# Thirty-five seven-product quads instead of twenty-six, with GpSimd making their sums, in an fp32 hybrid attention and state-space block

## The chip, the core and the metric

The kernel runs on one core of a Trainium2 chip. The time is the device time of one execution, in microseconds (us): the median of the runs, each a whole pass from inputs in device memory to the output. The core has five engines that run side by side, each with its own queue of instructions in a fixed order: TensorE (PE: matmuls; PEld: the loads of their stationary operand), VectorE (DVE), ScalarE (ACT), GpSimd (POOL) and SyncE (SP, which here only issues transfers). They wait for each other by semaphores.

## The reference

One block of a hybrid network on x of 256 rows and 2048 columns, in fp32:

```
hn   = rms_norm(x, norm_w)
q, k, v, z_a, z_s, xbc, dt, g_a, g_s = split(hn @ w_in)
o_a  = dilated_window_attention(q, k, v, three patterns) * silu(z_a)
y    = rms_norm(ssd_scan(conv(xbc), dt) * silu(z_s), ssm_norm_w)
m    = sigmoid(g_a) * (o_a @ w_attn_branch) + sigmoid(g_s) * (y @ w_ssm_branch)
out  = rms_norm(x + m @ w_out, final_norm_w)
```

The weights are about 63 million fp32 numbers, read once each; what takes the time is the matmuls with them.

## The kernel before, in words

**Three matmuls for one.** An fp32 product is made of operands split in a high part (what the matmul format keeps; ScalarE's copy) and a low part (VectorE's subtraction of the high part from the whole). A product is high x high + high x low + low x high: the helper `triple`, three matmuls of 128 x 128 with 512 columns. The activations are split once; every weight tile is split when it comes in. Weights come in units of 128 x 1024 (tag `w`, four buffers), and each unit's parts go to tiles `h` and `l` (four buffers each). `unit` does this for the plain case, lines 214 to 228.

**Phases.** First the projections for the state-space branch and its scan, then five large products in `gemm_pair` and others in `gemm_a` and `gemm_b`: ssm (4096 deep, output columns in two calls, 0 and 2, of 1024 each), v (columns 0 and 2), the gate ga (columns 2), then the attention heads with their projections, then attn (columns 0 in `gemm_pair`) and out (columns 0 and 2, in `gemm_pair`).

**Quads.** `gemm_pair` walks over the depth in steps of 2 x 128, a quad: two row blocks of the output by two column blocks of 512 by two depth blocks. A plain quad is 2 x 2 x 2 products, 24 matmuls. A quad listed in `S_QUADS` is made with seven products instead of eight (Strassen's way, in Winograd's form), 21 matmuls. For this its weights are stored in another order (units wa and wb), and sums are needed on both sides:

- of the weights: t13 (1024 wide, line 426), then two 512-wide sums in place in wb (lines 431 and 432). Four sets of high and low parts follow: a of wa, c of half of wb, t of t13, u of wb. The sets a and c take tiles from the ring `h`/`l` of four, t and u from a second ring `ht`/`lt` of two in the pool `mul`.
- of the left factor (activations): `turn_x`, lines 342 to 363: one sum of 512 columns, four of 128, then the split into `sx`. It is made once for each depth position and used by all calls that list it. Its temporary lies in a tile of its own.

Four accumulators hold the plain part, four more the extra products; `fold` (line 452) brings the latter together at a call's end, with two copies by ScalarE and four additions by VectorE.

**What sets the order.** A scheduler places the instructions of each engine at build time by its own model of their times; weight preparation is given a high priority (`L_AHEAD`), so that it runs ahead of the matmuls as far as buffers allow. On the chip each engine then keeps that order, whatever the real times are.

Of the kernel before, what the change touches and what calls it, by code (L numbers as in the profile page):

```python
# [9 lines left out]
F32 = mybir.dt.float32  # L10
F32R = mybir.dt.float32r
# [161 lines left out]
def hybrid_block(ctx: ExitStack, tc: tile.TileContext, wall, xt, x, pk_d, cst_d, fw_d, out):  # L173
# [33 lines left out]
    def load(n, cuts=(0, UNIT)):  # L207
        if n not in loaded:
            loaded[n] = stream.tile([P, UNIT], F32, name=f"w{n}", tag="w", bufs=W_BUFS)
        for a, b in zip(cuts, cuts[1:]):  # L210
            nc.sync.dma_start(loaded[n][:, a:b], wall[n, :, a:b])

    def unit(n, shape):
        if n not in loaded:
            load(n)
        w = loaded.pop(n)
        h = stream.tile([P, UNIT], F32R, name=f"h{n}", tag="h", bufs=H_BUFS)
        l = stream.tile([P, UNIT], F32R, name=f"l{n}", tag="l", bufs=H_BUFS)
        cuts = (0, UNIT // 2, UNIT) if n < N_FINE else (0, UNIT)
        with tc.high_priority(L_AHEAD) if n >= KT // UB else nullcontext():  # L220
            for a, b in zip(cuts, cuts[1:]):
                ac.activation(h[:, a:b], w[:, a:b], AF.Copy)  # L222
                ve.tensor_tensor(l[:, a:b], w[:, a:b], h[:, a:b].bitcast(F32), ALU.subtract)  # L223
# [117 lines left out]

    def turn_x(pool, bufs, temp, x, spare=0):


        sx = pool.tile([P, 2, 4 - spare, P], F32R, name=f"sx{now[0]}", tag="sx", bufs=bufs)
        a = temp[:, 0].rearrange("p (k i s) -> p k i s", k=2, i=2)
        s = temp[:, 1].rearrange("p (n s) -> p n s", n=4)
        xf = x.bitcast(F32)
        ve.tensor_tensor(a.rearrange("p k i s -> p k (i s)"), xf[:, :, :S], xf[:, :, S:], ALU.add)
        a11, a21, a12, a22 = a[:, 0, 0], a[:, 0, 1], a[:, 1, 0], a[:, 1, 1]  # L350
        ve.tensor_tensor(s[:, 0], a21, a22, ALU.add)
        ve.tensor_tensor(s[:, 1], a21, a11, ALU.subtract)
        ve.tensor_tensor(s[:, 2], s[:, 0], a11, ALU.subtract)
        ve.tensor_tensor(s[:, 3], a12, s[:, 2], ALU.subtract)
        parts = [(sx[:, 0, n], sx[:, 1, n]) for n in range(4 - spare)]
        if spare:
            own = x[:, 0, P:S], x[:, 0, S + P :]
            split(s[:, 0], *own)
            parts.insert(0, own)
        split(s[:, spare:], sx[:, 0], sx[:, 1])  # L360
        return parts

    def gemm_pair(tag, x_of, n_kt, sxs, swap, extra={}, close=1):
# [20 lines left out]
        for q in range(n_q):  # L384
# [27 lines left out]

            def hl(where, suffix, tags, bufs):
                return [
                    where.tile([P, UNIT], F32R, name=f"{t}{suffix}{n}", tag=t, bufs=bufs) for t in tags
                ]

            def part(src, h, l):
# [4 lines left out]
            with tc.high_priority(L_AHEAD):  # L423
                t13 = mul.tile([P, UNIT], F32, name=f"t13_{n}", tag="t13", bufs=1)
                b12 = wb[:, :512].unsqueeze(1).to_broadcast([P, 2, 512])
                ve.tensor_tensor(two(t13), b12, two(wa), ALU.subtract)
# [4 lines left out]
                ve.tensor_tensor(wb[:, :512], wa[:, 512:], t13[:, :512], ALU.subtract)  # L431
# [354 lines left out]
    mul = ctx.enter_context(tc.tile_pool(name="mul", bufs=1))  # L786
    mul.tile([P, MUL_PAD], F32, name="line", tag="line")

    def scale_gate():
# [17 lines left out]
    with tc.tile_pool(name="xp", bufs=1) as xp:  # L807
        sxs = {}
        for c in (0, 2):
            for q in S_QUADS[("ssm", c)]:  # L810
                if q not in sxs:
                    temp = xp.tile([P, 4, 512], F32, name=f"sxt_y{q}", tag="tmp", bufs=1)
                    sxs[q] = turn_x(xp, 6, temp, two_kts(yT[q // 8], q % 8), 1)
            es, prods = gemm_pair(
# [14 lines left out]
    sx_of_x = {}  # L829
    with tc.tile_pool(name="xt", bufs=1) as xtemp:  # L830
        for c in (0, 2):
            for q in S_QUADS[("v", c)]:
                if q not in sx_of_x:
                    temp = xtemp.tile([P, 2, 512], F32, name=f"sxt_x{q}", tag="tmp", bufs=1)
                    sx_of_x[q] = turn_x(xp, 3, temp, two_kts(XT, q))
            es, prods = gemm_pair(("v", c), lambda kt: XT[:, kt, :], KT, sx_of_x, c == 2)
            dst = blocks(vt, c)
            fold(prods, dst)
            for d, e in zip(dst, es):
                ve.tensor_tensor(d, e, d, ALU.add)  # L840
        es, prods = gemm_pair(("ga", 2), lambda kt: XT[:, kt, :], KT, sx_of_x, False)
        dst = blocks(th_a, 2)
        fold(prods, dst)
        for d, e in zip(dst, es):
            ve.tensor_tensor(d, e, d, ALU.add)
            ac.activation(d, d, AF.Tanh, scale=0.5)
    sxpool.close()
# [3 lines left out]
    with tc.tile_pool(name="att", bufs=2) as ap:  # L851
# [33 lines left out]
        def mix(h, pT, za):  # L885
# [8 lines left out]
            if h % 2 == 1 and q in S_QUADS[("attn", 0)]:  # L894
                temp = mul.tile([P, 2, 512], F32, name=f"sxt_o{q}", tag="t13", bufs=1)
                sx_of_o[q] = turn_x(xp, 3, temp, two_kts(oaT, q))

# [19 lines left out]
    with tc.tile_pool(name="fin", bufs=2) as fp:  # L917
# [38 lines left out]
        spare = big.tile([P, 8, 512], F32, name="spare", tag="yo0")  # L956
        sxs = {}
        for c0 in (0, 2):
            for n, q in enumerate(S_QUADS[("out", c0)]):
                if q not in sxs:  # L960
                    sxs[q] = turn_x(fp, 2, spare[:, 4 + 2 * n : 6 + 2 * n], two_kts(mT, q), 1)
            es, prods = gemm_pair(("out", c0), lambda kt: mT[:, kt, :], KT, sxs, c0 == 2, {}, 2 if c0 else 1)
            fold(prods, [spare[:, n] for n in range(4)])
            for i in range(2):
# [61 lines left out]
```

## Time and profile before

| | |
|---|---|
| median of 3 runs | 1397.56 us (1397.16 to 1398.91) |
| the profiled execution | 1397.75 us, span 1396.0 us |
| granted TensorE clock, mean | 0.998 |
| PE, PEld, DVE, ACT, POOL busy | 99%, 84%, 78%, 58%, 2% of the span |
| DMA | 272.33 MB, mean 195 GB/s |
| high parts in `unit`, L222 | 432 x 1050 ns on ACT |
| low parts in `unit`, L223 | 432 x 1212 ns on DVE |
| ssm, first to last matmul | 583.2 to 751 us |
| v; ga columns 2 | 751 to 834 us; 834 to 876 us |
| attn columns 0; out | 1213 to 1254 us; 1301 to 1386 us |

A row of a group names the line, the engine, the operation, output and inputs by the program's names, shape and count; behind the bar the busy time and the mean of one in ns; behind the next one the time that the engine was idle ahead of it, and for what. A row of the timeline begins with the start and the length in us; xN means N in a row. "Busy" of PE covers the pipeline, so one matmul's length is more than the distance of two.

### The profile page before, as it was taken

How to read it: one execution, taken by the hardware profiler on the slowest of the kernel's cores; microseconds unless marked ns; L12 is line 12 of the kernel's file. 1: busy time of each engine (PE TensorE's matmuls, PEld its weight loads, DVE VectorE, ACT ScalarE, POOL GpSimd, SP SyncE). 2: the span in 40 equal slices, each digit the busy share in tenths (PEclk: the TensorE clock that was granted, in tenths of full speed). 3: DMA queues.
4: the chain of work that ended last, by engine and by line, in shares of the span. 5: the costliest groups of instructions: out<-in, count | busy, mean ns of one | idle time of the engine just before them, and what ended most of it. 6: DMA issues, size and time to landing. Idle time of an engine off the chain costs nothing.

```text
span 1396.0 us, 19887 instructions
## 1 busy us (share of the span) xinstructions
PE 1383.5 (99%) x7308; PEld 1176.9 (84%) x7308; DVE 1088.9 (78%) x1622; ACT 809.8 (58%) x1258; POOL 30.5 (2%) x86
## 2 busy tenths in 40 slices
PE   9999999999999999999999999999999999999997
PEld 7888888888888888888888888888888888888885
DVE  6897888786788797798988988766666666487887
ACT  7756677675667585665554555544454544454453
POOL 1300000000000000000000000000000000000000
PEclk9999999999999999999999999999999999999999
DMA  8766665656565665556666565655555555667564
GB/s 325 245 193 190 194 207 172 217 181 200 179 206 182 202 197 173 185 179 213 193 210 198 188 218 183 220 172 174 171 172 176 181 169 175 199 211 251 171 196 136
DMA packets 78211, 272.33 MB, mean 195 GB/s; under 512 B 8801, under 2 KB 9377, under 8 KB 77729
## 3 DMA queue, kind: packets, MB, share of 16 engines
q1 hardware_dynamic: 77392, 269.88, 61.7%
q8 instruction: 57, 0.93, 0.3%
q10 hardware_dynamic: 720, 1.18, 0.2%
q14 instruction: 42, 0.34, 0.1%
HBM read 268.86 MB, written 2.16 MB: 194 GB/s over the span
## 4 chain that ended last, share of the span: by engine, by line
PE 91%; DVE 4%; DMA 3%; issue 1%; ACT 1%; SPq 0%; POOL 0%; POOLq 0%; DVEq 0%; ACTq 0%
PE ps_zs L261 8%; PE ps_xs L261 8%; PE ps_k L261 4%; PE ps_za L261 4%; PE ps_q L261 4%; PE ps_zs L262 4%; PE ps_xs L262 4%; PE ps_ssm L378 3%; PE ps_ssm L380 3%; PE ps_ssm L379 3%; DMA w<-in_wall 3%; PE ps_q L262 2%; PE ps_za L262 2%; PE ps_k L262 2%; PE ps_gs L338 2%; PE ps_gs L337 2%
## 5 line engine op out<-in xcount | busy, mean ns | idle before, releaser
L223 DVE TENSOR_TENSOR l<-w,h 128x1024 fp32r<-128x1024 f32 (+1 forms) x432 | 522.2, 1212 | 223.1 <-ACT h L222 220.0
L222 ACT ACTIVATE h<-w 128x1024 fp32r<-128x1024 f32 (+1 forms) x432 | 451.9, 1050 | 409.0 <-issue 99.1
L261 PE MATMUL ps_zs<-XT,h 128*128 128x512 f32 x496 | 175.8, 396 | 0.0
L261 PE MATMUL ps_xs<-XT,h 128*128 128x512 f32 x496 | 174.5, 394 | 0.0
L262 PE MATMUL ps_zs<-XT,l 128*128 128x256 f32 x496 | 139.2, 281 | 0.0
L262 PE MATMUL ps_xs<-XT,l 128*128 128x256 f32 x496 | 138.6, 279 | 0.0
L261 PEld LDWEIGHTS ps_zs<-XT,h 128*128 128x128 f32 x496 | 93.0, 188 | 22.6 <-issue 1.2
L261 PEld LDWEIGHTS ps_xs<-XT,h 128*128 128x128 f32 x496 | 93.0, 187 | 21.4
L262 PEld LDWEIGHTS ps_zs<-XT,l 128*128 128x128 f32 x496 | 93.6, 189 | 0.0
L262 PEld LDWEIGHTS ps_xs<-XT,l 128*128 128x128 f32 x496 | 93.5, 189 | 0.0
L261 PE MATMUL ps_q<-XT,h 128*128 128x512 f32 x256 | 92.4, 404 | 0.0
L261 PE MATMUL ps_za<-XT,h 128*128 128x512 f32 x256 | 89.7, 394 | 0.0
L261 PE MATMUL ps_k<-XT,h 128*128 128x512 f32 x256 | 89.7, 394 | 0.0
L262 PE MATMUL ps_q<-XT,l 128*128 128x256 f32 x256 | 71.3, 278 | 0.0
L262 PE MATMUL ps_za<-XT,l 128*128 128x256 f32 x256 | 71.0, 277 | 0.0
L262 PE MATMUL ps_k<-XT,l 128*128 128x256 f32 x256 | 71.0, 277 | 0.0
L379 PE MATMUL ps_ssm<-l,yT 128*128 128x512 f32 x168 | 65.2, 389 | 0.0
L380 PE MATMUL ps_ssm<-h,yT 128*128 128x512 f32 x168 | 65.1, 390 | 0.0
L378 PE MATMUL ps_ssm<-h,yT 128*128 128x512 f32 x168 | 57.5, 390 | 0.0
L261 PEld LDWEIGHTS ps_k<-XT,h 128*128 128x128 f32 x256 | 48.0, 188 | 11.3
L261 PEld LDWEIGHTS ps_za<-XT,h 128*128 128x128 f32 x256 | 48.0, 188 | 11.3
L261 PEld LDWEIGHTS ps_q<-XT,h 128*128 128x128 f32 x256 | 48.1, 188 | 10.9
(520 smaller groups left out, 2978.2 us busy)
## 6 DMA issues: line engine op xcount, KB each, us to landing
w<-in_wall SPq DMA_DIRECT2D x480, 512.0 KB, 3.8
acb<-acum_d SPq DMA_DIRECT2D x32, 256.0 KB, 3.5
th_s<-in_x SPq DMA_DIRECT2D x4, 512.0 KB, 8.0
vth<-in_x SPq DMA_DIRECT2D x1, 2048.0 KB, 9.3
early<-in_xt SPq DMA_DIRECT2D x7, 256.0 KB, 6.8
fw<-in_fw SPq DMA_DIRECT2D x1, 1024.0 KB, 5.7
out<-vth SPq DMA_DIRECT2D x4, 256.0 KB, 2.8
out<-vth ACTq DMA_DIRECT2D x4, 256.0 KB, 3.2
```

Of the source, the lines that this page charges most:

```text
L222: ac.activation(h[:, a:b], w[:, a:b], AF.Copy)
L223: ve.tensor_tensor(l[:, a:b], w[:, a:b], h[:, a:b].bitcast(F32), ALU.subtract)
L261: pe.matmul(acc, h[:, kk, :], m, start=(kt == 0), stop=False)
L262: pe.matmul(acc[:, S:], l[:, kk, :], m[:, :S], start=False, stop=(kt == KT - 1))
L337: pe.matmul(accs[i], xh, h[:, kk], start=(kt == 0), stop=False)
L338: pe.matmul(accs[i], xh, l[:, kk], start=False, stop=False)
L378: pe.matmul(acc, xh, h, start=start, stop=False)
L379: pe.matmul(acc, xh, l, start=False, stop=False)
L380: pe.matmul(acc, xl, h, start=False, stop=stop)
```

## The change

`S_QUADS` lists 35 quads instead of 26: 7 and 7 in ssm (5 and 6 before), 4 in each call of v and in ga (2, 3 and 3), 3 in attn (as before), 3 and 3 in out (2 and 2). The weights' layout follows the table.

The sums of the weights (t13 and the two behind it) and the five sums of `turn_x` move from VectorE to GpSimd, and with them the last two additions of every `fold` but the last. The splits stay with ScalarE and VectorE. The temporary of `turn_x` is now a tile of the tag t13, of which there is one, so that left factors and weight sums take turns in it. The two rings of high and low parts become one: `new_hl` hands out four pairs from `h`/`l` and then two from `ht`/`lt`, in turn, to plain and seven-product quads alike. Left factors are made ahead of a call (all four of v before its first call, those of out with all four parts kept), and the one of out's quad 6 inside the loop, at step 4.

```diff
 S_QUADS = {
-    ("ssm", 0): (5, 7, 9, 11, 13), ("ssm", 2): (3, 5, 7, 9, 11, 13),
-    ("v", 0): (4, 6), ("v", 2): (2, 4, 6), ("ga", 2): (2, 4, 6),
-    ("attn", 0): (2, 4, 6), ("out", 0): (3, 5), ("out", 2): (3, 5),
+    ("ssm", 0): (4, 6, 8, 9, 11, 12, 14), ("ssm", 2): (4, 6, 8, 9, 11, 12, 14),
+    ("v", 0): (2, 3, 5, 6), ("v", 2): (2, 3, 5, 6), ("ga", 2): (2, 3, 5, 6),
+    ("attn", 0): (2, 4, 6), ("out", 0): (3, 5, 6), ("out", 2): (2, 3, 5),
 }
...
+    more = []
+
+    def new_hl(n):
+
+        pool, tags, bufs = stream, "hl", H_BUFS
+        if more:
+            if more[1] % (H_BUFS + 2) >= H_BUFS:
+                pool, tags, bufs = more[0], ("ht", "lt"), 2
+            more[1] += 1
+        return [pool.tile([P, UNIT], F32R, name=f"{t}{n}", tag=t, bufs=bufs) for t in tags]
...
-    def turn_x(pool, bufs, temp, x, spare=0):
+    def turn_x(pool, bufs, x, spare=0):
 
 
         sx = pool.tile([P, 2, 4 - spare, P], F32R, name=f"sx{now[0]}", tag="sx", bufs=bufs)
+        temp = mul.tile([P, 2, 512], F32, name=f"sxt{now[0]}", tag="t13", bufs=1)
...
-        ve.tensor_tensor(a.rearrange("p k i s -> p k (i s)"), xf[:, :, :S], xf[:, :, S:], ALU.add)
+        gp.tensor_tensor(a.rearrange("p k i s -> p k (i s)"), xf[:, :, :S], xf[:, :, S:], ALU.add)
         a11, a21, a12, a22 = a[:, 0, 0], a[:, 0, 1], a[:, 1, 0], a[:, 1, 1]
-        ve.tensor_tensor(s[:, 0], a21, a22, ALU.add)
...
+        gp.tensor_tensor(s[:, 0], a21, a22, ALU.add)
+        gp.tensor_tensor(s[:, 1], a21, a11, ALU.subtract)
+        gp.tensor_tensor(s[:, 2], s[:, 0], a11, ALU.subtract)
+        gp.tensor_tensor(s[:, 3], a12, s[:, 2], ALU.subtract)
...
-                ve.tensor_tensor(two(t13), b12, two(wa), ALU.subtract)
-                ha, la = hl(stream, "a", "hl", H_BUFS)
+                gp.tensor_tensor(two(t13), b12, two(wa), ALU.subtract)
+                ha, la = new_hl(f"a{n}")
                 part(wa, ha, la)
-                hc, lc = hl(stream, "c", "hl", H_BUFS)
+                hc, lc = new_hl(f"c{n}")
                 part(wb[:, 512:], hc[:, :512], lc[:, :512])
-                ve.tensor_tensor(wb[:, :512], wa[:, 512:], t13[:, :512], ALU.subtract)
-                ve.tensor_tensor(wb[:, 512:], wb[:, 512:], wb[:, :512], ALU.subtract)
-                ht, lt = hl(mul, "t", ("ht", "lt"), 2)
+                gp.tensor_tensor(wb[:, :512], wa[:, 512:], t13[:, :512], ALU.subtract)
+                gp.tensor_tensor(wb[:, 512:], wb[:, 512:], wb[:, :512], ALU.subtract)
+                ht, lt = new_hl(f"t{n}")
                 part(t13, ht, lt)
-                hu, lu = hl(mul, "u", ("ht", "lt"), 2)
+                hu, lu = new_hl(f"u{n}")
                 part(wb, hu, lu)
...
-    def fold(prods, dst):
+    def fold(prods, dst, last=gp):
...
-        ve.tensor_tensor(d12, d12, d22, ALU.add)
-        ve.tensor_tensor(d22, d21, d22, ALU.add)
+        last.tensor_tensor(d12, d12, d22, ALU.add)
+        last.tensor_tensor(d22, d21, d22, ALU.add)
...
+        def last_set():
+            sxs[6] = turn_x(xp, 3, two_kts(mT, 6))
...
+            for q in S_QUADS[("out", c0)]:
+                if q not in sxs and q < 6:
+                    sxs[q] = turn_x(fp if c0 else xp, 1 if c0 else 3, two_kts(mT, q))
```

**VectorE before, at the first seven-product quad of ssm.** `t_` is t13, `w_` a weight unit, `l_` a low part of a plain quad, `la`, `lc`, `ltt`, `ltu` the low parts of the four sets, `sxt_y` the temporary of a left factor and `sx` its low part.

```order
L426 TENSOR_TENSOR t_203_6418<-w_6416,w_6414 128x1024
L353 TENSOR_TENSOR sxt_y_6169<-sxt_y_6169 128x128
L431 TENSOR_TENSOR w_6416<-w_6414,t_203_6418 128x512
L354 TENSOR_TENSOR sxt_y_6169<-sxt_y_6169 128x128
L223 TENSOR_TENSOR l_6383<-w_6380,h_6382 128x1024
L232 TENSOR_TENSOR yT_81<-sxt_y_6169,yT_81 128x128
L420 TENSOR_TENSOR ltt_6431<-t_203_6418,htt_6430 128x1024
L420 TENSOR_TENSOR la_6421<-w_6414,ha_6420 128x1024
L232 TENSOR_TENSOR sx_6170<-sxt_y_6169,sx_6170 128x384
L420 TENSOR_TENSOR lc_6425<-w_6416,hc_6424 128x512
```

The first quad's sums stand between the steps of the second left factor; the other left factors follow later, among the quads.

**GpSimd with the change, at the same place.** `sxt` is the temporary of a left factor; lines 432, 437 and 438 are the weight sums. The first of these left factors waits for the last row of the scan.

```order
L363 TENSOR_TENSOR sxt_6225<-sxt_6225 128x128
L364 TENSOR_TENSOR sxt_6225<-sxt_6225 128x128
L365 TENSOR_TENSOR sxt_6225<-sxt_6225 128x128
L432 TENSOR_TENSOR t_201_6404<-w_6402,w_6400 128x1024
L437 TENSOR_TENSOR w_6402<-w_6400,t_201_6404 128x512
L438 TENSOR_TENSOR w_6402<-w_6402 128x512
L432 TENSOR_TENSOR t_205_6485<-w_6483,w_6481 128x1024
L437 TENSOR_TENSOR w_6483<-w_6481,t_205_6485 128x512
```

All seven left factors of ssm now stand ahead of the first quad's sums, this one as the last of them; then the quads follow one another.

**TensorE with the change, where it first asks for t13.** `htt_6416` and `ltt_6417` are t13's parts; `pp_` are the extra accumulators.

```order
L389 MATMUL ps_ssm_0_6235<-hc_6491,yT_81 128x512
L390 MATMUL ps_ssm_0_6235<-lc_6492,yT_81 128x512
L391 MATMUL ps_ssm_0_6235<-hc_6491,yT_81 128x512
L389 MATMUL pp_ssm_1_6397<-htt_6416,yT_81 128x512
L389 MATMUL pp_ssm_3_6399<-htt_6416,sx_6158 128x512
L390 MATMUL pp_ssm_1_6397<-ltt_6417,yT_81 128x512
L391 MATMUL pp_ssm_1_6397<-htt_6416,yT_81 128x512
L390 MATMUL pp_ssm_3_6399<-ltt_6417,sx_6158 128x512
```

132 matmuls of ssm stand ahead of the first of them, among them the sets a and c of quads 4 and 6 and most of the plain quads up to 5. PE keeps this order.

More of the change, by code (lines that the diff above doesn't have):

```diff
@@ L216, in unit @@
         w = loaded.pop(n)
[L217 to L218 removed]
+        h, l = new_hl(n)
         cuts = (0, UNIT // 2, UNIT) if n < N_FINE else (0, UNIT)
@@ L411, in gemm_pair @@
             wa, wb = loaded.pop(n), loaded.pop(n + 1)
[L413 to L416, printed above, removed]
             def part(src, h, l):
@@ L787, in hybrid_block @@
     mul.tile([P, MUL_PAD], F32, name="line", tag="line")
+    more.extend((mul, 0))
     def scale_gate():
@@ L811, in hybrid_block @@
                 if q not in sxs:
-                    temp = xp.tile([P, 4, 512], F32, name=f"sxt_y{q}", tag="tmp", bufs=1)
-                    sxs[q] = turn_x(xp, 6, temp, two_kts(yT[q // 8], q % 8), 1)
+                    sxs[q] = turn_x(xp, 7, two_kts(yT[q // 8], q % 8), 1)
             es, prods = gemm_pair(
@@ L829, in hybrid_block @@
     sx_of_x = {}
[L830 to L842, printed above, removed]
+    for q in S_QUADS[("v", 0)]:
+        sx_of_x[q] = turn_x(xp, 4, two_kts(XT, q))
+    for c in (0, 2):
+        es, prods = gemm_pair(("v", c), lambda kt: XT[:, kt, :], KT, sx_of_x, c == 2)
+        dst = blocks(vt, c)
         fold(prods, dst)
@@ L845, in hybrid_block @@
             ve.tensor_tensor(d, e, d, ALU.add)
-            ac.activation(d, d, AF.Tanh, scale=0.5)
+    es, prods = gemm_pair(("ga", 2), lambda kt: XT[:, kt, :], KT, sx_of_x, False)
+    dst = blocks(th_a, 2)
+    fold(prods, dst)
+    for d, e in zip(dst, es):
+        ve.tensor_tensor(d, e, d, ALU.add)
+        ac.activation(d, d, AF.Tanh, scale=0.5)
     sxpool.close()
@@ L894, in mix @@
             if h % 2 == 1 and q in S_QUADS[("attn", 0)]:
-                temp = mul.tile([P, 2, 512], F32, name=f"sxt_o{q}", tag="t13", bufs=1)
-                sx_of_o[q] = turn_x(xp, 3, temp, two_kts(oaT, q))
+                sx_of_o[q] = turn_x(xp, 3, two_kts(oaT, q))
         for h in range(NH):
@@ L957, in hybrid_block @@
         sxs = {}
+        def last_set():
+            sxs[6] = turn_x(xp, 3, two_kts(mT, 6))
         for c0 in (0, 2):
[L959 to L963, printed above, removed]
+            for q in S_QUADS[("out", c0)]:
+                if q not in sxs and q < 6:
+                    sxs[q] = turn_x(fp if c0 else xp, 1 if c0 else 3, two_kts(mT, q))
+            es, prods = gemm_pair(("out", c0), lambda kt: mT[:, kt, :], KT, sxs, c0 == 2, {} if c0 else {4: last_set}, 2 if c0 else 1)
+            fold(prods, [spare[:, n] for n in range(4)], ve if c0 else gp)
             for i in range(2):
```

3 lines of the change are left out of this document (removed).

## The prediction

> **What bounds the kernel now.** I read the page's busy shares first, then the stretches in which the seven-product quads run, then what VectorE does there.
>
> ```profile
> PE 1383.5 (99%) x7308; PEld 1176.9 (84%) x7308; DVE 1088.9 (78%) x1622; ACT 809.8 (58%) x1258; POOL 30.5 (2%) x86
> ```
>
> ```profile
> 583.00:667.00 84.00, 84.00 (x377) 69.54 (x375) 75.72 (x110) 49.54 (x60) 0.96 (x1) 1.00 0.59 185
> 667.00:751.00 84.00, 84.00 (x372) 69.58 (x371) 75.03 (x86) 45.53 (x49) 0.00 (x0) 1.00 0.65 210
> 751.00:793.00 42.00, 42.00 (x187) 34.75 (x186) 37.55 (x51) 22.50 (x26) 0.00 (x0) 1.00 0.62 197
> 1304.00:1348.00 44.00, 44.00 (x199) 36.36 (x198) 40.58 (x55) 25.61 (x36) 1.19 (x1) 1.00 0.57 181
> ```
>
> The second fence is the table by stretch: length, then busy time of PE, weight loads, DVE, ACT, POOL, then clock and DMA. TensorE is never idle in the two ssm halves, in v and in the first out half, at a granted clock of 1.00; VectorE is busy for some 90% of each. So what is taken off PE there shortens the program one for one, as long as VectorE's work, in whose place part of GpSimd's now steps, still keeps up. GpSimd does next to nothing.
>
> ```profile
> 1357.14 0.39 PE L379 MATMUL ps_out<-l,mT 128*128 128x512 f32 x1
> 1359.41 0.39 PE L380 MATMUL ps_out<-h,mT 128*128 128x512 f32 x1
> ```
>
> These are ten matmuls apart in the timeline: 2.27 / 10 = 0.227 us each (the 0.39 includes the pipeline). A plain quad has 24 of them, 5.45 us, one with seven products 21, 4.77 us.
>
> **The change part by part.** *Matmuls.* Nine more quads save 27 matmuls: 6.1 us. I make the sum against the profiled execution's 1397.75 us (1396.0 of span and 1.75 around it; 0.2 above the runs' median): 1391.6 with nothing lost.
>
> *What VectorE gives up.*
>
> ```profile
> L426 DVE TENSOR_TENSOR t<-w,w 128x1024 f32<-128x1024 f32 x26 | 31.8, 1224 | 17.4 <-DMA w<-in_wall 17.3
> L420 DVE TENSOR_TENSOR la<-w,ha 128x1024 fp32r<-128x1024 f32 x26 | 31.7, 1219 | 3.5 <-ACT ha L419 3.4
> L420 DVE TENSOR_TENSOR lc<-w,hc 128x512 fp32r<-128x512 f32 x26 | 17.8, 685 | 0.2 <-ACT hc L419 0.2
> L431 DVE TENSOR_TENSOR w<-w,t 128x512 f32<-128x512 f32 x26 | 17.8, 685 | 0.0
> 574.50 2.35 DVE L223 TENSOR_TENSOR l<-w,h 128x1024 fp32r<-128x1024 f32 x2
> ```
>
> Two 1024-wide subtractions in a row take 2.35, so one costs 2.35 - 1.21 = 1.14 of VectorE, and a 512-wide one by the same overlap 0.61. A seven-product quad cost it four of the first (three low parts and t13) and three of the second: 6.4 us against PE's 4.77. With the sums gone it is 3 x 1.14 + 0.61 = 4.0, a plain quad 2.3. Taken alone, VectorE would now keep up with any density of such quads. ScalarE's share of a quad does not change.
>
> *What GpSimd takes on.* No wide two-input operation of GpSimd stands in the trace. The nearest rows are its copies, with VectorE beside them.
>
> ```profile
> 39.12 0.19 POOL L508 COPY cst<-h 128x1 f32<-128x1 f32 x1
> 48.09 1.24 POOL L535 COPY rxs<-h 128x1 f32<-128x1 f32 x1 [8.78 <-ACT h L222]
> 49.39 0.40 POOL L536 COPY rxs<-early 128x256 f32<-128x256 f32 x1
> 59.33 1.29 POOL L536 COPY rxs<-early 128x256 f32<-128x256 f32 x1
> 46.44 0.88 DVE L234 SCALAR_TENSOR_TENSOR XT<-early,pk,XT 128x256 fp32r<-128x256 f32 x2
> 48.06 1.23 DVE L223 TENSOR_TENSOR l<-w,h 128x1024 fp32r<-128x1024 f32 x1 [0.75 <-ACT h L222]
> 59.14 1.22 DVE L223 TENSOR_TENSOR l<-w,h 128x1024 fp32r<-128x1024 f32 x1
> 60.27 1.02 DVE L234 SCALAR_TENSOR_TENSOR XT<-early,pk,XT 128x256 fp32r<-128x256 f32 x2
> ```
>
> Two things are to be seen. Alone, a one-column copy takes 0.19 and a 256-column one 0.40: 0.21 / 255 = 0.82 ns a column, and 0.19 fixed. But the copy that starts at 48.09, 0.03 behind a VectorE subtraction, takes 1.24: it ends at 49.33 where the subtraction ends at 49.29. The 256-wide copy at 59.33 ends 0.26 behind the subtraction that ends at 60.36, and the pair of VectorE operations that follows takes 1.02 rather than 0.88. So the two engines took turns on two-input VectorE work: GpSimd waited for the whole of VectorE's instruction, and VectorE then waited for GpSimd's copy. Every low part of this kernel (l from w and h) is such a VectorE instruction.
>
> For GpSimd's two-input sum I bound the column between 0.82 ns (as the copy) and 1.65 (two operands read one after the other), and take 1.65, since it reads twice what the copy does. A quad's sums, 1024 + 512 + 512 columns, then take 3.4 us, or 3.95 with three fixed parts; the sums of one left factor, 512 + 4 x 128 columns, 1.7 or 2.65; the two additions of a fold 1.7 or 2.1.
>
> The Trainium skill, GPSIMD Engine Reference, Elementwise (side-by-side cycle accounting), measures 4497 ns for a 2048-column addition, 2.2 ns a column; worked out from it as an estimate, a quad's sums would be 4.5 us and the loss summed below 84 rather than 57. The Trainium skill, SBUF: State Buffer, Who interferes with whom, says that a VectorE instruction with two SBUF inputs and a GpSimd instruction that reads SBUF shut each other out for the length of an instruction; the 1.24 for 0.19 agrees, and that a long GpSimd instruction holds VectorE as long is shown by no row here.
>
> *Whether it fits.* If they take turns, a seven-product quad needs 4.0 + 3.4 = 7.4 us of the two together (7.95 with the fixed parts exposed) where PE needs 4.77; a left factor 1.7 + 0.6 = 2.3 (3.2). By stage, in us, fixed parts hidden and, in brackets, exposed:
> ssm columns 0: 7 x 7.4 + 9 x 2.3 + 7 x 2.3, and 6 for the scan's last rows, is 94.6 against PE's 82.4: 12 lost (23).
> ssm columns 2: 7 x 7.4 + 9 x 2.3 + 4 is 76.5 against 82.4, but quads 8 to 12 (four with seven products, one plain) need 31.9 against 24.5, and six tile pairs hold a lead of about 5 (one seven-product quad takes four of them, 4.77 of PE): 2 lost (4.5).
> v columns 0: 4 x 7.4 + 4 x 2.3 + 4 x 2.3 + 4 is 52 against 40.9: 11 lost (17).
> v columns 2 and ga: 40.5 each against 40.9, with two pairs of neighbours at 14.8 against 9.5 less the lead: 2 each (4 each).
> attn: 35.4 against 41.6: none.
> out columns 0: its stretch above has 40.58 of VectorE, of which two old quads, six plain and two left factors are 31, so 10 of other work; 3 x 7.4 + 5 x 2.3 + 3 x 2.3 + 10 is 50.6 against 41.6: 9 lost (13).
> out columns 2: even in sum, quads 2 and 3 are neighbours: 4 lost (6).
> Together 42 (71); I take the middle, 57, since GpSimd's fixed part hides behind VectorE only where VectorE has something else ready, and most of what is queued there waits for the very sums that GpSimd is making.
>
> *The first quad, whatever the ports do.* The temporary of a left factor is now t13, in a pool that opens when the scan's last row is written, and there is one of it.
>
> ```profile
> 583.26 0.87 DVE L691 SCALAR_TENSOR_TENSOR y<-xs,pk,yp 128x256 f32<-128x256 f32 x2
> 591.81 0.87 DVE L234 SCALAR_TENSOR_TENSOR yT<-y,pk,yT 128x256 fp32r<-128x256 f32 x2
> 597.17 0.52 ACT L230 ACTIVATE sx<-sxt_y 128x384 fp32r<-128x384 f32 x1 [1.50 <-DVE sxt_y L354]
> 597.73 0.56 DVE L232 TENSOR_TENSOR sx<-sxt_y,sx 128x384 fp32r<-128x384 f32 x1
> 605.17 1.05 ACT L419 ACTIVATE ha<-w 128x1024 fp32r<-128x1024 f32 x1
> L378 PE MATMUL ps_ssm<-h,yT x168: 387/389/499, 583.2 to 750.2; 128*128 128x512 f32 x168
> ```
>
> All seven left factors stand on GpSimd ahead of the first quad's sums. Each takes 1.8 (0.82 ns) to 2.65, then 0.52 and 0.56 for its parts before t13 is free, and some 0.3 of hand-overs (0.06 lies between the copies that end at 49.33 and start at 49.39): 3.2 to 4.1. From 592.7, seven end at 615 to 621, t13 and its high part at 617 to 624. PE asks for them 132 matmuls behind 583.2, at 613.2: 4 to 11 lost, which the 57 contains. What stands behind: VectorE's later low parts, and PE's own order.
>
> Costing nothing: the folds' last additions (PE is already in the next stage; the last fold stays on VectorE), and weight tiles held longer, unless the two loads of the next quad then come late, which I leave inside the range.
>
> **The rivals.** *The engines do not take turns on long instructions* (the 0.14 that VectorE lost to a copy is all there is). Only the start-up is lost, 4 to 11, and up to 5 at v's four left factors: 1396 to 1408, about 1402. The copies' 1.24 speaks against it.
> *All is hidden*: 1391.6, faster. It holds if a left factor takes under (613.2 - 592.7 - 2.1) / 7 = 2.6 us and the engines overlap; the low bound of 3.2 and the copies speak against it, VectorE's relief of 2.4 us a quad for it.
> *The chain decides, not the sum*: one t13 lets no two quads overlap. Its three sums, high part and low part in series are 3.95 + 1.05 + 1.22 + 0.3, and 1.8 for three waits of half a VectorE instruction: 8.3 a quad. 35 x (8.3 - 4.77) is 124; less what leads win back, some 30: 1490.
>
> **How the numbers follow.** Turns taken, 0.65: 1391.6 + 57 = 1449; 42 and 71 give 1434 and 1463, and with some 10 to 15 more on each side for leads and waits that I could only estimate its own range is 1425 to 1480. Start-up alone 0.16, all hidden 0.11, the chain 0.08. A measurement here tells 0.2% (2.8 us) from no change, so start-up alone gives 0.06 to no change and 0.10 to slower; faster 0.11, same 0.06, slower 0.83. The range from 1396 to 1480 leaves out all hidden and the chain.
>
> **What would show it.** Right: PE idle at the first htt of ssm and in each stage by about the losses above, low parts of 1.2 us that last 2 to 3 beside GpSimd's sums or start that much later, sums that last longer than 1.9 by VectorE's instructions. Wrong: GpSimd's 1024-wide sums near 1 to 2 us with VectorE's low parts undisturbed, or PE without gaps.

## The result

The changed kernel takes 1509.37 us (median; 1509.31 to 1510.87), the one before 1398.02 beside it: 1.080 times as long, interval 1.0785 to 1.0812. The profiled execution has a span of 1507.6 us at a mean granted clock of 0.976. The forecast was 1449 us with a range of 1396 to 1480: slower as forecast, but by 111 us instead of 51, and outside the range. Against the 1391.6 that fewer matmuls alone would give, 118 us were lost where 57 were expected.

The page of the changed kernel, busy times and the row of granted clock by slice:

```profile
PE 1418.4 (94%) x7281; PEld 1175.9 (78%) x7281; DVE 1129.3 (75%) x1481; ACT 826.3 (55%) x1279; POOL 356.8 (24%) x295
PEclk9999999999999999799998799999999999999998
```

PE has 27 matmuls fewer, as the change says, and is busy 35 us longer. VectorE has 141 instructions fewer, and is busy 40 us *longer*. GpSimd went from 30 to 357 us. The stretches of ssm (two rows) and v, of the changed kernel (length, busy time of PE, weight loads, DVE, ACT, POOL, clock, DMA):

```profile
583.00:667.00 84.00, 61.96 (x250) 45.73 (x251) 56.67 (x56) 38.40 (x50) 53.99 (x49) 0.90 0.35 110
667.00:751.00 84.00, 76.60 (x324) 59.59 (x323) 64.76 (x49) 39.42 (x44) 44.18 (x22) 1.00 0.56 178
797.00:919.00 122.00, 96.12 (x362) 70.57 (x361) 86.32 (x68) 50.60 (x57) 68.15 (x43) 0.87 0.45 140
```

In the first 84 us PE does 250 matmuls, against 377 in the same stretch before. VectorE starts 56 instructions where it started 110, and these 56 take 57 us. The groups by shape of GpSimd and then of VectorE say why (count, busy time, mean of one in ns, idle time ahead and for what):

```profile
L432 POOL TENSOR_TENSOR t<-w,w 128x1024 f32<-128x1024 f32 x35 | 89.7, 2562 | 147.2 <-DMA w<-in_wall 123.7 <-DVE vth L465 11.2 <-DVE lt L426 4.8
L438 POOL TENSOR_TENSOR w<-w 128x512 f32<-128x512 f32 x35 | 70.5, 2016 | 26.4 <-DVE lc L426 17.9 <-DVE ltc L426 7.0
L437 POOL TENSOR_TENSOR w<-w,t 128x512 f32<-128x512 f32 x35 | 64.9, 1854 | 2.5
```

```profile
L426 DVE TENSOR_TENSOR lu<-w,hu 128x1024 fp32r<-128x1024 f32 x23 | 42.2, 1835 | 38.7 <-ACT hu L425 38.6
L426 DVE TENSOR_TENSOR la<-w,ha 128x1024 fp32r<-128x1024 f32 x21 | 37.4, 1783 | 2.4 <-ACT ha L425 2.4
L426 DVE TENSOR_TENSOR lc<-w,hc 128x512 fp32r<-128x512 f32 x21 | 30.0, 1428 | 5.1 <-ACT hc L425 5.1
```

The low part `la` of a seven-product quad took 1219 ns before and takes 1783 now, the half-wide `lc` 685 and now 1428. GpSimd's half-wide sums take 1.85 to 2.02, though alone they take 1.27, as its timeline at the first quad shows (start, length, operation, and the wait ahead of it):

```profile
592.65 1.29 POOL L360 TENSOR_TENSOR sxt<-yT 128x512 f32<-128x512 f32 x1 [69.94 <-DVE yT L244]
628.30 0.46 POOL L365 TENSOR_TENSOR sxt<-sxt 128x128 f32<-128x128 f32 x1
629.98 2.34 POOL L432 TENSOR_TENSOR t<-w,w 128x1024 f32<-128x1024 f32 x1 [1.23 <-DVE sx L242]
632.40 1.27 POOL L437 TENSOR_TENSOR w<-w,t 128x512 f32<-128x512 f32 x1
633.75 2.13 POOL L438 TENSOR_TENSOR w<-w 128x512 f32<-128x512 f32 x1
```

The first row opens the first of seven left factors and the second row ends the last of them: 36 us, about 5 each. The undisturbed durations are 2.34 us for 1024 columns, 1.27 for 512 and 0.45 for 128. PE, in its waits and in its timeline behind the longest of them:

```profile
PE pp_ssm L389 <- ACT htt L425: 16.5, 1, 16.5
PE pp_v L389 <- ACT ht L425: 11.4, 1, 11.4
```

```profile
633.47 0.79 PE L389 MATMUL pp_ssm<-htt,yT 128*128 128x512 f32 x1 [16.51 <-ACT htt L425]
...
635.39 0.63 PE L391 MATMUL pp_ssm<-htt,yT 128*128 128x512 f32 x1
635.82 0.63 PE L390 MATMUL pp_ssm<-ltt,sx 128*128 128x512 f32 x1
636.25 0.63 PE L391 MATMUL pp_ssm<-htt,sx 128*128 128x512 f32 x1
...
639.68 0.39 PE L391 MATMUL pp_ssm<-htu,sx 128*128 128x512 f32 x1
639.91 0.39 PE L390 MATMUL ps_ssm<-ltu,yT 128*128 128x512 f32 x1
```

The first product with a sum of weights waited 16.5 us, and the matmuls behind it start 0.43 us apart, not 0.227, for the next six microseconds.

By stage, from the first to the last matmul of each in the timelines (the first column is PE's need: matmuls by 0.227):

| us | need | after | lost | forecast lost |
|---|---|---|---|---|
| ssm | 164.8 | 213.8 | 49 | 14 to 27.5 |
| v | 81.8 | 122.0 | 40 | 13 to 21 |
| ga columns 2 | 40.9 | 51 | 10 | 2 to 4 |
| attn | 87.6 | 90.8 | 3 | 0 |
| out | 83.2 | 97.2 | 14 | 13 to 19 |

What stood to be explained: why ssm, v and ga lost two to three times their forecast or more. The theories were: *turns* (VectorE's and GpSimd's two-input work shut each other out, so the sum of both counts); *start* (left factors, one behind the other through the one t13, hold up the first quad, and the clock falls behind the stall); *chain* (a quad's weight tile is held from its load to the last low part, and there are four); and *density* (35 quads are too many whoever makes the sums).

### The profile page after: what moved, and what is told of

The parts are those of the page before. It is cut to its first block, busy times and chain, and to the rows that moved or that the text cites. A ratio compares the mean times of both kernels' runs of the same rounds, so it can differ in the third digit from the quotient of the medians.

```text
span 1507.6 us, 20103 instructions
## 1 busy us (share of the span) xinstructions
PE 1418.4 (94%) x7281; PEld 1175.9 (78%) x7281; DVE 1129.3 (75%) x1481; ACT 826.3 (55%) x1279; POOL 356.8 (24%) x295
## 4 chain that ended last, share of the span: by engine, by line
PE 65%; POOL 11%; DVE 10%; issue 6%; DMA 5%; ACT 3%; POOLq 0%; SPq 0%; DVEq 0%; ACTq 0%
PE ps_zs L271 8%; PE ps_xs L271 8%; DMA w<-in_wall 5%; PE ps_za L271 4%; PE ps_k L271 4%; PE ps_q L271 4%; PE ps_zs L272 4%; PE ps_xs L272 4%; POOL w L438 3%; POOL t L432 3%; PE ps_q L272 2%; PE ps_za L272 2%; PE ps_k L272 2%; PE ps_gs L348 2%; PE ps_gs L347 2%
## 5 line engine op out<-in xcount | busy, mean ns | idle before, releaser
L233 DVE TENSOR_TENSOR l<-w,h 128x1024 fp32r<-128x1024 f32 (+1 forms) x348 | 433.3, 1250 | 153.0 <-ACT h L232 150.7
L232 ACT ACTIVATE h<-w 128x1024 fp32r<-128x1024 f32 (+1 forms) x348 | 363.6, 1049 | 268.2 <-issue 55.6
L432 POOL TENSOR_TENSOR t<-w,w 128x1024 f32<-128x1024 f32 x35 | 89.7, 2562 | 147.2 <-DMA w<-in_wall 123.7
L233 DVE TENSOR_TENSOR lt<-w,ht 128x1024 fp32r<-128x1024 f32 x66 | 85.2, 1295 | 50.7 <-ACT ht L232 50.6
L232 ACT ACTIVATE ht<-w 128x1024 fp32r<-128x1024 f32 x66 | 69.6, 1060 | 67.8 <-PE ps_k L271 44.3
L271 PE MATMUL ps_k<-XT,ht 128*128 128x512 f32 x256 | 89.7, 394 | 0.0
L619 POOL MEMSET raw_x<- 128x4 f32 x31 | 3.2, 103 | 316.8 <-DVE cv_B L629 155.9
L438 POOL TENSOR_TENSOR w<-w 128x512 f32<-128x512 f32 x35 | 70.5, 2016 | 26.4 <-DVE lc L426 17.9
L426 DVE TENSOR_TENSOR lu<-w,hu 128x1024 fp32r<-128x1024 f32 x23 | 42.2, 1835 | 38.7 <-ACT hu L425 38.6
L272 PE MATMUL ps_k<-XT,lt 128*128 128x256 f32 x256 | 71.0, 277 | 0.0
```

The costliest lines, as they stand in the source:

```text
L271: pe.matmul(acc, h[:, kk, :], m, start=(kt == 0), stop=False)
L272: pe.matmul(acc[:, S:], l[:, kk, :], m[:, :S], start=False, stop=(kt == KT - 1))
L426: ve.tensor_tensor(l, src, h.bitcast(F32), ALU.subtract)
L432: gp.tensor_tensor(two(t13), b12, two(wa), ALU.subtract)
L438: gp.tensor_tensor(wb[:, 512:], wb[:, 512:], wb[:, :512], ALU.subtract)
L619: gp.memset(raw[:, 0:4], 0.0)
```

## The experiments

### GpSimd's three jobs, taken back one at a time

Each run gives one job back to VectorE and keeps the 35 quads.

First the sums of weights (35 x 3):

```diff
-gp.tensor_tensor(two(t13), b12, two(wa), ALU.subtract)
+ve.tensor_tensor(two(t13), b12, two(wa), ALU.subtract)
 # and the two sums into wb likewise
```

> The three sums of weights of all 35 quads go back to VectorE (105 instructions); left factors and folds stay on GpSimd, the table and the ring of six stay. Nothing is left out. If the main loss in ssm and v is GpSimd's slow sums with their chain (sum on GpSimd, high part on ScalarE, low part on VectorE, only then a free weight tile and its load), the rows in which GpSimd waits for a weight tile (123.7 us before 16 of its sums) go, and what stays is the late start (about 16 us in ssm, 11 in v, with the low clock behind each some 10 more): 1391.6 + 16 + 11 + 10 to 20 of VectorE's longer quads, 1430 to 1450. If it is the number of seven-product quads that costs, with 6.4 us of VectorE each against PE's 4.77, the loss stays: 1480 to 1510.

Measured: 1451.8 us, 58 less than the change and just above the first range. VectorE's low part `lu` takes 1222 ns here, about what the 1024-wide subtractions took before, and 1835 in the change. The late starts stay, as expected: PE waits 15.3 and 10.8 us.

Then the sums of left factors alone:

```diff
-gp.tensor_tensor(a.rearrange(...), xf[:, :, :S], xf[:, :, S:], ALU.add)
+ve.tensor_tensor(a.rearrange(...), xf[:, :, :S], xf[:, :, S:], ALU.add)
 # and s[:, 0] to s[:, 3] likewise
```

> The sums of left factors go back to VectorE, with the one temporary tile kept; sums of weights and folds stay on GpSimd. Nothing is left out. If the chain of the weights is the main loss and the start-up the smaller one, the waits at the first seven-product quad go (16.5 us in ssm, 11.4 in v) and some of the slow clock behind them: 1509 less 28 to 40, 1470 to 1482. If the start-up and the clock that falls behind it were the main loss, 1430 or below. If GpSimd's left factors cost nothing beside the rest, 1505 or more.

Measured: 1496.4, only 13 less, in none of the three ranges. Both waits were forecast to go, and they stayed at 13.5 us in ssm and 8.0 in v: VectorE, too, has to pass every left factor through t13 before the first sum of weights.

Then all of it, folds included:

> All of GpSimd's new work goes back to VectorE: sums of weights, left factors and folds. What stays of the change is the table of 35 quads, the ring of six and the one temporary tile. Nothing is left out. If GpSimd is the cause, the time is near the one before: 6.1 us less of matmuls, 27 to 40 us more of VectorE over ssm, v, ga and out, most of it beside PE's work: 1395 to 1415. If the table is the cause whichever engine makes the sums (6.4 us of VectorE a quad against 4.77 of PE in stages where nearly every second k pair is a quad), over 1430.

Measured: 1437.1 (1.0281, 1.0264 to 1.0298), beyond the range for GpSimd as the only cause, and in the one for the table: 40 us above the kernel before, with GpSimd nearly as idle as it was there (40 us busy against 30). In this order of steps the sums of weights on GpSimd cost 58, its other work 15, and the rest of the change 40; in another order the shares differ.

### What the 40 consist of

The left factors of ssm, v and ga get a temporary of their own, as before the change:

```diff
-        temp = mul.tile([P, 2, 512], F32, name=..., tag="t13", bufs=1)
+        if temp is None:
+            temp = mul.tile([P, 2, 512], F32, name=..., tag="t13", bufs=1)
...
+                    temp = xp.tile([P, 4, 512], F32, name=..., tag="tmp", bufs=1)
+                    sxs[q] = turn_x(xp, 7, two_kts(yT[q // 8], q % 8), 1, temp)
```

> As the kernel with all sums back on VectorE (35 quads, ring of six, 1437 us), but the left factors of ssm, v and ga have a temporary of their own again instead of t13. Nothing is left out. There PE waited 12.2 us for the first htt of ssm and 8.2 for the first ht of v, and the granted clock fell behind each. If the one t13 is the cause (all left factors must pass through it before the first quad's sum of weights may), both waits go with their low clock: 1437 less 35 to 45, 1392 to 1402. If the cause is that VectorE has 35 dear quads and their left factors to do, whichever tile it uses, 1425 or more.

Measured: 1427.1 (1.0218, 1.0200 to 1.0236). Sharing t13 was worth 10 us, not 35 to 45; the second expectation was the right one.

The ring of six by itself, with the 26 quads:

> The ring of six alone: the table of before (26 quads), all sums on VectorE, the left factors of ssm, v and ga in a temporary of their own; of the change only the ring of six (and the last turned factors of out in t13) is left. Nothing is left out. If the ring costs or wins nothing, 1396 to 1400, and the 30 us by which 35 quads with all sums on VectorE are slower come from the quads. If handing out high and low parts from one ring holds something up, 1405 or more.

Measured: 1398.1 (1.0005, 0.9996 to 1.0014). The ring costs nothing. So nine more quads cost 29 us, although they save 6 and although each sum is where it was.

Where, was asked by taking two of them out of v's first half, which then has seven products in quads 5 and 6 alone. The left factors of these two are also made first:

```diff
-    ("v", 0): (2, 3, 5, 6), ...
+    ("v", 0): (5, 6), ...
...
-    for q in S_QUADS[("v", 0)]:
+    for q in (5, 6, 2, 3):
```

> As the kernel with 35 quads, all sums on VectorE and left factors in their own temporary (1427 us), but the first half of v has seven products in quads 5 and 6 alone, not in 2, 3, 5 and 6 (33 quads); its four left factors are still made there. Nothing is left out. By VectorE's sum for that half (4 x 6.4 + 4 x 2.3 + 4 x 2.3 + 4 = 48 against PE's 40.9; with two, 2 x 6.4 + 6 x 2.3 + 4 x 2.3 + 4 = 39.8 against 42.3) it wins 7 less 1.4 for six more matmuls: about 1421. If the loss of 20 us that v showed comes from the first two quads, whose left factors VectorE can only make once ssm's last fold and the first weights are done, 1410 to 1416. If v's place of the quads doesn't matter, 1427 or more.

Measured: 1415.2 (1.0121, 1.0101 to 1.0141), 12 less, twice what the sum over the half gives and in the second range, that of the first two quads. The waits of PE from ssm's end to ga, with 35 quads first and then with 33:

```profile
PE ps_v L390 <- ACT sx L240: 5.6, 2, 3.3
PE ps_v L390 <- ACT hu L426: 2.1, 1, 2.1
PE ps_v L391 <- DVE ltc L427: 2.0, 1, 2.0
```

```profile
PE ps_v L390 <- ACT sx L240: 1.4, 1, 1.4
```

The likely reason, argued and not shown apart: VectorE has ssm's last fold, v's first weights and four left factors to make when PE asks for quad 2. With the same edit GpSimd's version was asked too:

> The changed kernel with the same edit: the first half of v has seven products in quads 5 and 6 alone (33 quads), GpSimd makes all sums. Nothing is left out. With the durations that its own trace shows, a quad needs 4.0 of VectorE and 4.9 of GpSimd, a left factor 3.1 and 0.8: by the sum of turns the half needs 4 x 8.9 + 4 x 2.3 + 4 x 3.9 + 4 = 64 before and 2 x 8.9 + 6 x 2.3 + 4 x 3.9 + 4 = 51 now, so it wins 13 less 2: about 1498. If the first quads' late start and the low clock behind it are more than that sum, 1480 to 1490.

Measured: 1497.5, as the sum of turns says with the durations of the trace. That is weak evidence for the sum: the same edit won as much, 12, in the kernel in which VectorE makes all sums, where the sum gave 6.

Last, two quads more where VectorE's sum says that there is room, in the kernel before:

```diff
-    ..., ("ssm", 2): (3, 5, 7, 9, 11, 13), ... ("ga", 2): (2, 4, 6),
+    ..., ("ssm", 2): (3, 5, 7, 9, 11, 13, 14), ... ("ga", 2): (2, 4, 5, 6),
```

> The kernel before with two more quads only, where VectorE has room by its sum: ssm columns 2 seven instead of six, ga four instead of three, with one more left factor each. VectorE then needs 7 x 6.4 + 9 x 2.3 + 2 x 2.3 + 4 = 74 of PE's 82.4 in ssm columns 2, and 4 x 6.4 + 4 x 2.3 + 2.3 + 4 = 41.1 of 40.9 in ga. Nothing is left out. If VectorE's sum by stage decides, six matmuls fewer, 1.36 us: 1395.5 to 1397. If neighbouring quads (13 and 14, 5 and 6) cost more than the sum says, 1399 to 1405.

Measured: 1398.5 (1.0008, 1.0000 to 1.0017). That lies between the two ranges: the 1.4 us of fewer matmuls were not won. Two more quads at these places gain nothing, and no version that was run beats the kernel before.

### Do the two engines shut each other out?

The forecast rested on GpSimd's copies alone. Here the kernel before gets GpSimd sums that nothing uses and nothing waits for, so that no chain can play a part:

```diff
+                if idles:
+                  idle = idles[0]
+                  gp.tensor_copy(idle[:, 0:1], ha[:, 0:1].bitcast(F32))
+                  gp.tensor_tensor(idle, cst[:, :1024], cst[:, :1024], ALU.add)
+                  # and two 512-wide additions
```

> The kernel before, with work added that nothing uses: in ssm, v and ga (19 of its 26 quads) GpSimd makes, behind each quad's first high part, one copy of a column, one 128x1024 and two 128x512 additions of constants into a tile of their own. No engine waits for them. If VectorE's subtractions and GpSimd's sums shut each other out, VectorE loses up to 19 x 4.9 = 93 us there, of which some 29 (a tenth of the 292 us of these stages) were idle: 1420 to 1460, with low parts of 1.8 us as in the changed kernel. If only GpSimd is slowed and VectorE isn't, or if what costs in the changed kernel is that others wait for the sums, 1397 to 1402.

Measured: 1454.9 us (1.0413, 1.0390 to 1.0435), in the first range: 57.5 us, 3.0 for each of the 19 quads. VectorE's groups in that run, from 583 to 876 us, which holds 16 of the 19:

```profile
L426 DVE TENSOR_TENSOR t<-w,w 128x1024 f32<-128x1024 f32 x16 | 30.9, 1933 | 10.7 <-DMA w<-in_wall 10.5
L420 DVE TENSOR_TENSOR la<-w,ha 128x1024 fp32r<-128x1024 f32 x16 | 30.1, 1882 | 1.2 <-ACT ha L419 1.2
L420 DVE TENSOR_TENSOR lc<-w,hc 128x512 fp32r<-128x512 f32 x16 | 19.6, 1224 | 0.0
```

and how the two look side by side, GpSimd's timeline first, then VectorE's:

```profile
694.66 1.89 POOL L440 TENSOR_TENSOR idle<-cst 128x1024 f32<-128x1024 f32 x1
696.63 2.16 POOL L441 TENSOR_TENSOR idle<-cst 128x512 f32<-128x512 f32 x1
698.75 2.27 POOL L442 TENSOR_TENSOR idle<-cst 128x512 f32<-128x512 f32 x1
```

```profile
694.78 2.85 DVE L426 TENSOR_TENSOR t<-w,w 128x1024 f32<-128x1024 f32 x1 [0.77 <-DMA w<-in_wall]
697.55 2.32 DVE L420 TENSOR_TENSOR la<-w,ha 128x1024 fp32r<-128x1024 f32 x1
```

VectorE's `t` is issued 0.12 behind GpSimd's first sum, which ends at 696.55; 1.08 later, at 697.63, `t` ends. GpSimd's second sum was issued at 696.63, begins to work when `t` ends, and is done 1.16 later, at 698.79; `la` ends 1.08 behind that. One instruction of the one, then one of the other: turns, in both directions, for the 512 and 1024 columns seen here. The size is not to be set equal to the 58 of GpSimd's sums of weights in the change, since VectorE still made its own sums here, and for 19 quads; but turns alone, where nobody waits for the sums, are enough for a loss like that one.

The changed kernel's own trace has the pace of the turns as well. In the middle of ssm two seven-product quads and a plain one follow one another, and GpSimd begins the group anew at

```profile
646.54 3.01 POOL L432 TENSOR_TENSOR t<-w,w 128x1024 f32<-128x1024 f32 x1 [3.87 <-DMA w<-in_wall]
666.72 2.40 POOL L432 TENSOR_TENSOR t<-w,w 128x1024 f32<-128x1024 f32 x1 [4.83 <-DMA w<-in_wall]
687.50 2.39 POOL L432 TENSOR_TENSOR t<-w,w 128x1024 f32<-128x1024 f32 x1 [6.06 <-DMA w<-in_wall]
```

20.2 and 20.8 us apart. VectorE's and GpSimd's work for such a group is 2 x (4.0 + 4.9) + 2.3 = 20.1 us by their undisturbed durations; PE needs 15.0. The two kinds of work fill the time one behind the other, and while GpSimd waits for its load, VectorE makes low parts. The pace alone would not tell turns from a chain through the same instructions; the runs with more weight tiles, further down, bear on that.

### Start and chain

If the start is a loss of its own, taking the left factors out of t13 must help the changed kernel itself (same edit as above, sums on GpSimd):

> The changed kernel, with all its sums on GpSimd, but the left factors of ssm, v and ga in a temporary of their own instead of t13. Nothing is left out. If passing through the one t13 is what makes both starts late, the waits of 16.5 and 11.4 go with some 10 to 15 of low clock: 1509 less 30 to 42, 1467 to 1480, and what is left over 1392 is GpSimd's sums by themselves. If GpSimd is late because its left factors are slow (5 us each, one after the other), 1500 or more.

Measured: 1509.8, no gain at all, though the long waits went: the longest waits of PE are now

```profile
PE ps_v L390 <- ACT hu L426: 6.2, 3, 3.7
PE ps_v L391 <- DVE lu L427: 5.1, 2, 4.1
```

The loss had only moved. The stretch after ssm's first quad in this run:

```profile
625.00:670.00 45.00, 34.36 (x118) 23.07 (x117) 41.04 (x25) 17.88 (x24) 43.70 (x29) 0.89 0.41 125
```

In 45 us VectorE shows 41 us of busy time with 25 instructions, GpSimd 44 with 29: each was working or shut out by the other nearly all the time. That fits a price that is paid wherever the left factors are made: what is not done ahead of the first quad is done behind it.

The chain was tested with more weight tiles. In the changed kernel, two more during v and ga:

```diff
+    wide.extend((xp, -1))   # of every six loads, two go to tiles "wx" of xq
```

> The changed kernel with two more weight tiles (six instead of four) during v and ga. Nothing is left out. If the chain limits the middle of the stages (sum on GpSimd, high and low part, only then a free weight tile, then its load), GpSimd's waits for loads in v and ga shrink and so do the gaps of PE there: 1509 less 10 to 25, 1484 to 1499. If GpSimd's and VectorE's turns limit it, the loads come earlier and the time stays within 5 us of 1509.

Measured: 1503.8, 5.6 less, just outside the range for the turns and far from the one for the chain. GpSimd's waits for loads in v and ga, three of 6 us, are gone; one of 9.8 us, ahead of ga's first quad, is new. Then the kernel with the table of 26 quads, sums on GpSimd:

> The table of before, 26 quads, with the sums on GpSimd and the ring of six as in the change; v's left factors are made for the quads of both its halves as before. Nothing is left out. If each seven-product quad pays a price of its own on GpSimd (some 111/35 = 3.2 us), 26 cost 82 us: about 1480. If the loss comes from quads that stand next to each other (a pair of them every 20 us in the middle of ssm), spreading them lets the chain of weights recover: 1420 to 1445, start-up included. If only the nine added quads cost, about 1400.

Measured: 1457.9 (1.0432, 1.0411 to 1.0453), between the two expectations. Its GpSimd shows a regular pace in ssm:

```profile
635.45 2.40 POOL L432 TENSOR_TENSOR t<-w,w 128x1024 f32<-128x1024 f32 x1 [6.11 <-DMA w<-in_wall]
648.02 2.40 POOL L432 TENSOR_TENSOR t<-w,w 128x1024 f32<-128x1024 f32 x1 [6.25 <-DMA w<-in_wall]
660.42 2.40 POOL L432 TENSOR_TENSOR t<-w,w 128x1024 f32<-128x1024 f32 x1 [6.07 <-DMA w<-in_wall]
```

A seven-product quad and a plain one take 12.4 us here, PE needs 10.2, and each time GpSimd sits 6 us waiting for a load. That looks like the chain. So this kernel got a fifth weight tile in ssm and two more in v and ga:

> The kernel with 26 quads and GpSimd's sums (1458 us), with five weight tiles instead of four in ssm and six in v and ga. Nothing is left out. There ssm's quads of seven products alternate with plain ones, and GpSimd begins its sums every 12.4 us, after waiting some 6 us for a load each time, while PE needs 4.77 + 5.45 = 10.2 for the pair, and the turns of VectorE and GpSimd 4.0 + 2.3 + 4.9 = 11.2. A pair takes four weight tiles, as many as there are. If the weight tile is what sets the 12.4 (sums 6.2, high and low part 2.3, then the load 4 into the freed tile), the period falls to 11 to 11.5 with a fifth tile and below in v with six: 1458 less 10 to 20, 1438 to 1448. If the turns alone set it, the loads come earlier, the waits for them go, and the period stays near 12.4: 1452 or more.

Measured: 1449.1 (1.0370, 1.0349 to 1.0390), 9 less.

```profile
712.12 2.66 POOL L437 TENSOR_TENSOR t<-w,w 128x1024 f32<-128x1024 f32 x1 [1.97 <-DMA w<-in_wall]
714.85 2.15 POOL L442 TENSOR_TENSOR w<-w,t 128x512 f32<-128x512 f32 x1
719.97 2.14 POOL L443 TENSOR_TENSOR w<-w 128x512 f32<-128x512 f32 x1 [2.96 <-DVE lc L431]
724.01 2.72 POOL L437 TENSOR_TENSOR t<-w,w 128x1024 f32<-128x1024 f32 x1 [1.91 <-DMA w<-in_wall]
735.86 2.82 POOL L437 TENSOR_TENSOR t<-w,w 128x1024 f32<-128x1024 f32 x1 [1.79 <-DMA w<-in_wall]
```

GpSimd now waits 2 us for its load instead of 6, and for VectorE's `lc` as well; the pace goes from 12.4 to 11.9, not to 10.2. ssm stays as long as it was (200.8 and 200.7; its first sum began 2.6 us later, at 626.05 rather than 623.42), v and ga win 9. The 6 us of waiting for a load were mostly a symptom. The result lies between the two expectations (1438 to 1448, and 1452 or more), nearer to the chain's; by the pace it is turns first, weight tiles second.

## Why the prediction was right and wrong

**Right.** The matmuls (7281, 27 fewer). That the engines take turns, the step that had the chance of 0.65: the idle sums show it in both directions. attn at almost nothing (3 measured). Out at 13 to 19 was met by 14, but with prices that were too low, so that this is luck. Rivals "start-up alone" (1402) and "all is hidden" (1391.6) are out. "The chain decides" gave 1490, the number nearest to the result, by quads that wait for each other at the one t13. No run gave t13 a second tile (the run of 1509.8 took only the left factors out of it), so this is not tested directly. The trace speaks against it: of the 147.2 us that GpSimd idled ahead of its 35 sums into t13, 4.8 ended with the low part `lt` that frees t13.

**The step that failed first is a mis-sized term: GpSimd's column.** It was bounded between 0.82 ns and 1.65, from a copy, and 1.65 was taken. The trace of the change has 2.34 us for 1024 columns and 0.45 for 128: (2.34 - 0.45) / 896 = 2.1 ns, and 0.18 fixed, above the upper bound. So a quad's sums take 2.34 + 2 x 1.27 = 4.9 us, not 3.4 to 3.95, and a left factor's 1.27 + 4 x 0.45 = 3.1, not 1.7 to 2.65. A quad needs 4.0 + 4.9 = 8.9 of the two engines, a left factor 3.9 with its parts on VectorE. With these prices, the prediction's own sum by stage, neighbours and leads as there, is 34 + 8 (ssm) + 23 + 8 (v) + 8 (ga) + 0 (attn) + 18 + 7 (out) = 106 instead of 42 to 71: 1498. So this one term makes up most of what was missing between 57 and 118. The Trainium skill, GPSIMD Engine Reference, Elementwise (side-by-side cycle accounting), had 2.2 ns a column, and the sums of the change agree with it. The prediction's estimate by the page, 84, was the better one of the two. Not every two-input sum costs as much: the idle sum of 1024 columns above, which adds one operand to itself, took 1.89 us, 1.7 ns a column behind the same 0.18. Why was not found out. The bound from one-input copies did not hold for the two-input sums of the change.

**The second: what the plain pairs were let to pay.** With the right prices the sum still has 42 for ssm (49 measured), 31 for v (40) and 8 for ga (10), and 25 for out, where 14 were measured. In the first halves of ssm, v and out it lets a stage's first and last plain pairs pay for the quads between; for the neighbours elsewhere it grants a lead. A likely reason against it, argued and not shown by a run of its own, is that PE can be fed only a few units ahead, by four weight tiles and a ring of six. Counted from the first quad to the last alone, with nothing paid by the plain pairs outside:

| us | both engines | PE | lost |
|---|---|---|---|
| ssm, each half (4 to 14) | 7 x 8.9 + 4 x 2.3 = 71.5 | 7 x 4.77 + 4 x 5.45 = 55.2 | 16.3 |
| v, each half, and ga (2 to 6) | 4 x 8.9 + 2.3 = 37.9 | 24.5 | 13.4 |
| attn (2 to 6) | 3 x 8.9 + 2 x 2.3 = 31.3 | 25.2 | 6 |
| out, each half | 3 x 8.9 + 2.3 = 29.0 | 19.8 | 9.2 |

With the waits at the starts, 16.5 in ssm and 11.4 in v, that is ssm 49 (measured 49), v 38 (40), ga 13 (10), attn 6 (3), out 18 (14): 125 against some 116. This was worked out after the result, and the two waits in it are measured, not forecast; they stand for the turns of the left factors, since the run without these waits lost as much. It was not made for ssm of the 26 quads on GpSimd, and gives there: from quad 5 to 13, 5 x 8.9 + 4 x 2.3 = 53.7 against PE's 45.7, from 3 to 13 of the second half 6 x 8.9 + 5 x 2.3 = 64.9 against 55.9, one left factor of 3.9, and the wait at its start, 9.5: 30. The sum over whole halves gives some 12. Measured: 200.8 less the 167.4 that ssm took before, 33. The forecast also called VectorE able to "keep up with any density of such quads", which was meant for 4.0 us a quad; it never asked what 35 quads do at the 6.4 of before. There the nine quads more cost 29 us, 12 of them by v's first two, and two quads more than before win nothing.

**The first quad.** Forecast at 617 to 624 with 4 to 11 us lost; PE got it at 633.47 and waited 16.5, again by the column's price (3.1 us of GpSimd for a left factor rather than 1.8 to 2.65) and by turns. But without that wait the time is the same, so it is where the loss shows and no loss of its own.

**Weight tiles held longer**, costed at nothing "unless the two loads of the next quad then come late": they did, with 44.0 us of GpSimd's waiting in ssm and 18.4 in v and ga (123.7 over the whole program). More tiles were worth 5.6 us in v and ga, and 9 with 26 quads. In ssm with 35 quads no run tried more of them, so their share there stays open.

**Not foreseen: the clock.** Behind PE's first long gap matmuls are 0.43 us apart for some 6 us. The Trainium skill, TensorE: Matmul & The Clock Gate, Part 1 (the HAM clock gate), says that the array falls to half its clock after a short idle window; the 0.43 behind the 16.5 us wait agrees. PE's busy time is 1418.4 in the change and 1390.2 with the same 7281 matmuls and VectorE's sums (own temporary). That difference of 28 us holds both slow matmuls and lone ones that show their whole pipeline, and how much of it lengthened the program was not told apart: where the two other engines set the pace, a slow PE may cost nothing. That stays open.

## What to carry to other kernels

In this kernel VectorE's two-input work and GpSimd's were one resource, not two: add their times before moving such work from the one to the other, with GpSimd at twice VectorE's time for a column (2.1 ns against the 1.05 between its 1224 ns for 1024 columns and 685 for 512). A stage's surplus before its dense stretch may not be there to spend inside it; a sum from the first costly unit to the last was nearer here than one over whole stages. And when a long wait is named (for a load, for a first product), take it away once before believing it: here two of them, 16.5 us once and 6 us each time, went, and the program won nothing by the one and 9 us by the other.

## What was not expected of the hardware

A one-column copy by GpSimd waited far longer than one turn. In the run with the idle sums, GpSimd's timeline:

```profile
617.85 11.84 POOL L439 COPY idle<-ha 128x1 f32<-128x1 f32 x1 [4.47 <-ACT ha L419]
694.39 0.18 POOL L439 COPY idle<-ha 128x1 f32<-128x1 f32 x1 [26.80 <-ACT ha L419]
```

and VectorE's, where its run of instructions ends:

```profile
629.37 0.27 DVE L232 TENSOR_TENSOR yT<-sxt_y,yT 128x128 fp32r<-128x128 f32 x1
630.82 1.93 DVE L420 TENSOR_TENSOR la<-w,ha 128x1024 fp32r<-128x1024 f32 x1 [1.17 <-ACT ha L419]
```

The same copy takes 0.18 us at 694.39 and 11.84 at 617.85; of the 19 copies three took more than 4 us. In those 11.84 us VectorE ran without a pause, one instruction starting before the one ahead of it had ended, until 629.64; the copy ends at 629.69. GpSimd's two-input sums, in the same run, never waited for more than one VectorE instruction. Why the copy does not get a turn was not found out.
